# Ordering the norm chains' TensorE work behind later projection matmuls, in a two-layer diffusion backbone

## The chip, the cores and the metric

One core of a Trainium2 chip (trn2). The metric is the device time of one execution in microseconds (us). Engine names in the rows: PE is TensorE's matmuls, PEld its weight loads, DVE VectorE, ACT ScalarE, POOL GpSimd, SP SyncE, which issues the transfers.

## The reference, cut to what matters

512 latent tokens and 256 context tokens, 1024 features wide, pass two layers. Each layer is a mixer (layer 0: neighbourhood attention beside an mLSTM; layer 1: multi-head latent attention, MLA) and a gated ConvFFN, and each result is normalized twice: once as a sandwich norm of the branch, once as the norm that feeds the next projection.

```python
x = x + g1 * rms_norm(yx, norm_g[l, 1])
hx = modulate(rms_norm(x, norm_g[l, 2]), sh2, sc2)
x = x + g2 * rms_norm(conv_ffn(hx, ffn_w_up[l], ffn_conv_w[l], ffn_conv_b[l], ffn_w_down[l]), norm_g[l, 3])
...
def rms_norm(x, g):
    xf = x.astype(jnp.float32)
    y = xf * lax.rsqrt(jnp.mean(xf * xf, axis=-1, keepdims=True) + EPS)
    return (y * g.astype(jnp.float32)).astype(x.dtype)
```

The context tokens go through the same weights in layer 0, and only latent tokens leave layer 1.

## The kernel before, in words

Features lie on the partitions, in KD = 8 tiles of 128 (index k or m), tokens on the free axis. Every fp32 operand of a projection is split into a high and a low part, so each product is three matmuls: high weights (`whi`) by high data, high weights by low data, low weights (`wlo`) by high data. ACT makes `whi`, DVE `wlo`, from a transferred `wraw`.

The tokens of a projection are worked as segments: SX (512 latent columns) and SC (256 context columns) in layer 0's output projection and front of its FFN; SH[0] and SH[1] (256 latent columns each) and SC1 in the last part of layer 0's down projection and in layer 1. When all eight tiles of a segment are projected, its norm chain (`YNorm.chain`, L443; `RawNorm.chain`, L489) is put on a list, and the loops of the next segment trace a few of its steps after each of their own tiles (`step`, L381; `until`, L390, traces what is left). The chain of a segment is, in order:

1. column sums of squares over all features (`sums4`, L395, tiles `ysum` and `pss`, groups of four small matmuls; `pssy` for the wide segment);
2. ACT copies the sums (`srow`), four or two `psc` matmuls select and turn them (`sums_bc`, L405), DVE copies them to `rv`, POOL raises them to a power (`ry`), three short DVE instructions refine `ry`;
3. PE spreads `ry` over the partitions by transposes (`bcasts`, L367, `bcast`, L231), into `bcy` for the sandwich norm and `bcm` for the second norm;
4. for each k DVE scales the branch by `bcy` (a scalar_tensor_tensor on `acc`), DVE or POOL adds it to the stream (`x`), ACT squares, and after k = 3 and k = 7 four `pss` matmuls add up;
5. steps 2 and 3 again for `bcm`, and for each k DVE, ACT and in some k POOL make the high and low part `h` that the next projection reads.

A RawNorm chain (last down projection of layer 0) makes the unscaled `h` within its step 4, by ACT and DVE, and its `bcm` only gives a factor that is applied later.

Around the chains stand `yps` matmuls (output projection, L1195 to L1219), `puf` (the first up projections of an FFN, `front`, L1266), `pu` and `pd` (its steady middle), `pdl` (the last group of the down projection, L1325; its results go through PSUM tiles with two buffers and are added to `acc` by one DVE instruction each), and `qps`, `kps`, `kvp` (the projections of MLA). A scheduler of the language orders the instructions of every engine from what is traced and from its own estimate of times; each engine then runs its own list in that order. An order can be asked for between two instructions (`tc.issue_after`, used in `sums4`). In MLA the keys of a head are split into parts by `split_keys0`, the second head's after the first tile of scores of head 0 was traced (L1658).

Of the kernel before, what the change touches and what calls it, by code (L numbers as in the profile page):

```python
# [18 lines left out]
TX = 512  # L19
TC = 256  # L20
T = TX + TC
# [43 lines left out]
def hybrid_backbone_kernel(ctx: ExitStack, tc: tile.TileContext, *aps):  # L65
    nc = tc.nc
    V, S, G, PE = nc.vector, nc.scalar, nc.gpsimd, nc.tensor
    a = dict(zip(_DEV, aps))
    out = aps[len(_DEV)]
# [68 lines left out]
    def instr(i):  # L138
        return getattr(i, "ins", i)

    def mm(o, l, r, start, stop):
        return PE.matmul(out=o, lhsT=l, rhs=r, start=start, stop=stop)  # L142

    def tr(o, i):
        PE.transpose(out=o, in_=i, identity=ident[0:i.shape[0], 0:i.shape[0]])  # L145

    def act(o, i, func=AF.Copy, **kw):
        S.activation(out=o, in_=i, func=func, **kw)  # L148
# [41 lines left out]
    def proj(o, w, x, cols, ks=tuple(range(KD)), first=True, last=True):  # L190

        whi, wlo = w
        xhi, xlo = x
        for lo, hi, oo in cols:
            for k in ks:
                wh = whi[:, k * 128:(k + 1) * 128]
                wl = wlo[:, k * 128:(k + 1) * 128]
                oa = o[:, oo:oo + hi - lo]
                mm(oa, wh, xhi[:, k, lo:hi], first and k == ks[0], False)
                mm(oa, wh, xlo[:, k, lo:hi], False, False)  # L200
                mm(oa, wl, xhi[:, k, lo:hi], False, last and k == ks[-1])

    def proj_steps(o, w, x, cols):
        for c in cols:
# [24 lines left out]
        return y  # L229

    def bcast(o, col):  # L231
        tr(o, col.to_broadcast([128, 128]))

    def colsum(pss, sq, j, k, nk, first):
        mm(pss[:, j:j + 1], sq, ones_c, first, k == nk - 1)
# [131 lines left out]
    def bcasts(rs, n, name):  # L367
        bc = (ps_a if n > 4 else ps_c)("bc" + name)
        for j in range(n):
            bcast(bc[:, j * 128:(j + 1) * 128], rs[:, j:j + 1])  # L370
        return bc

    def sq_cols(pss, src, w, first, last):
        sq = sqp.tile([128, 512], F32, tag="sq", name="sq")
        act(sq[:, :w], src, AF.Square)
        for j in range(w // 128):
            mm(pss[:, j:j + 1], sq[:, j * 128:(j + 1) * 128], ones_c, first and j == 0, last and j == w // 128 - 1)

    chains = []

    def step(n):  # L381

# [7 lines left out]
    def until(sg):  # L390

        while any(c[0] == sg for c in chains):
            step(1)

    def sums4(ps, w, srcs, first, last):  # L395

        def one(i):
            return PE.matmul(out=ps[32 * i:32 * i + 32, 0:w], lhsT=ones32, rhs=srcs[i], start=first, stop=last,
                             tile_position=(0, 32 * i))
        n_ = len(srcs) - 1  # L400
        with tc.issue_after(instr(one(n_))):
            for i in range(n_):
                one(i)

    def sums_bc(ps, sg, name):  # L405

        row = scratch("srow")
        act(row[:, 0:sg.w], ps[:, 0:sg.w])
        psc = ps_c("psc")
        for j in range(sg.nt):  # L410
            mm(psc[:, j:j + 1], row[:, j * 128:(j + 1) * 128], sel4[:, 0:1], True, True)
        return rstd_bc(psc, sg.nt, D, name)

    class YNorm:
# [811 lines left out]
    def ffn(l, segs, osegs, parts, xs, h, accp, acc, Gt, groups, mod=None, done=lambda sg, k: None,  # L1226
# [5 lines left out]
        with ExitStack() as fs:  # L1232
# [58 lines left out]
            def down_mm(o, js, wu, m, sg):  # L1291
                for j in js:
                    whi, wlo = wu[j]
                    xh, xl = hid[j]
                    wh, wl = whi[:, m * 128:(m + 1) * 128], wlo[:, m * 128:(m + 1) * 128]
                    c0, c1 = sg.po, sg.po + sg.w
                    mm(o, wh, xh[:, c0:c1], j == js[0], False)
                    mm(o, wh, xl[:, c0:c1], False, False)
                    mm(o, wl, xh[:, c0:c1], False, j == js[-1])

            full = segs if pw > 512 else [Seg(n, 0, 0, 0)]

# [238 lines left out]
    with ExitStack() as l1b:  # L1541
# [112 lines left out]
                tt(V, h1lo[k], mixb[k], fr(h1hi[k]), ALU.subtract)  # L1654

        wv1 = wload(a["w_ukv"][1])
        for i, _ in enumerate(scores(0)):
            if i == 0:  # L1658
                for lo, hi in ((0, TX), (TX, T)):
                    split_keys0(1, lo, hi)  # L1660
            if i < 2:
                prep_q(i + 1)
            if i < NT // 2:
                prep_v(0, [i])
# [179 lines left out]
```

## Time and profile before

| | us |
|---|---|
| time, median of three runs | 1801.6 (1799.39 to 1803.42) |
| profiled execution | 1800.14 |
| its span, first to last instruction | 1798.2 |
| PE busy | 1732.4 (96%) |
| DVE busy | 1177.8 (66%) |
| ACT busy | 749.0 (42%) |
| POOL busy | 254.4 (14%) |
| mean granted clock of PE | 0.990 |

Busy time is the union of an engine's instructions. The views used are the page, the waits of an engine (who was waited for, in total, how often, and the longest), busy time by windows (with the granted clock), and the timeline, whose rows give the start, the duration, the instruction and in brackets the idle time ahead of it. A row of the timeline with x2 or x3 joins neighbours of one kind and gives their common duration. The span is 1.9 us shorter than the execution.

### The profile page before, as it was taken

To read this page: it belongs to the slowest core of one execution; us is meant where nothing else is said; L and a number is where in the kernel's file an instruction comes from. 1 tells how busy PE (TensorE), PEld (TensorE's weight loads), DVE (VectorE), ACT (ScalarE), POOL (GpSimd) and SP (SyncE) were. 2 spreads that over 40 slices of the span, in tenths; PEclk is the share of its full clock that TensorE was granted. 3 is DMA by queue.
4 is the path that set the end of the run, shared out by engine and by line. 5 is a ranking of instruction groups with operands and counts; after the bars stand their busy time and mean duration, and the time that the engine had idled before them with its cause. 6 is when DMAs were issued, how large, how long until landed. Compare 5 with 4: busy or idle time off the path is not lost.

```text
span 1798.2 us, 26707 instructions
## 1 busy us (share of the span) xinstructions
PE 1732.4 (96%) x10498; PEld 1454.3 (81%) x10498; DVE 1177.8 (66%) x2308; ACT 749.0 (42%) x1300; POOL 254.4 (14%) x304
## 2 busy tenths in 40 slices
PE   6999999999999999999999999999999999999997
PEld 4777877887878888888888878788878888888885
DVE  3384577559266686777764657788884574556555
ACT  3333345445344422232221335577784454333242
POOL 1000024225320000000000002344451200000001
PEclk8999999999999999999999999999999999999999
DMA  9344232113313343444331311000012133324221
GB/s 309 109 136 141 83 107 93 54 53 124 100 36 94 117 127 118 135 125 135 119 98 60 91 39 49 24 13 13 13 36 85 48 108 94 92 84 134 76 94 48
DMA packets 63261, 162.40 MB, mean 90 GB/s; under 512 B 6272, under 2 KB 19792, under 8 KB 63136
## 3 DMA queue, kind: packets, MB, share of 16 engines
q1 hardware_dynamic: 61616, 156.52, 27.7%
q0 software_dynamic: 1376, 4.04, 0.6%
q8 instruction: 83, 1.36, 0.3%
q14 instruction: 42, 0.34, 0.1%
q10 hardware_dynamic: 144, 0.13, 0.0%
HBM read 158.57 MB, written 2.10 MB: 89 GB/s over the span
## 4 chain that ended last, share of the span: by engine, by line
PE 70%; DVE 5%; ACT 2%; POOL 2%; issue 2%; DMA 1%; DVEq 0%; POOLq 0%; ACTq 0%
PE pu L142 29%; PE pd L142 14%; PE sp L142 4%; PE yps L142 4%; PE puf L142 3%; PE pdl L142 3%; PE pt L145 2%; PE qp L142 2%; PE ot L142 2%; PE vp L142 1%; PE kp L142 1%; DVE acc L157 1%; PE ops L142 1%; DVE wlo L151 1%; PE ptp L145 1%
## 5 line engine op out<-in xcount | busy, mean ns | idle before, releaser
L148 ACT ACTIVATE whi<-wraw 128x1024 fp32r<-128x1024 f32 x186 | 195.5, 1058 | 465.7 <-PE pu L142 210.0
L151 DVE TENSOR_TENSOR wlo<-wraw,whi 128x1024 fp32r<-128x1024 f32 x184 | 226.3, 1234 | 222.4 <-ACT whi L148 222.1
L142 PE MATMUL pu<-h,whi 128*128 128x256 f32 (+1 forms) x1280 | 315.4, 337 | 0.0
L142 PEld LDWEIGHTS pu<-h,whi 128*128 128x128 f32 x1280 | 219.8, 190 | 26.3 <-issue 1.0
L142 PE MATMUL pd<-hid,whi 128*128 128x512 f32 (+1 forms) x864 | 232.6, 357 | 1.6 <-DVE acc L151 1.5
L142 PE MATMUL pu<-h,wlo 128*128 128x512 f32 (+1 forms) x640 | 215.2, 336 | 0.0
L142 PEld LDWEIGHTS pd<-hid,whi 128*128 128x128 f32 x864 | 152.5, 189 | 28.2 <-DVE acc L151 3.9
L151 POOL TENSOR_TENSOR ry<-rv,mhalf 128x2 f32<-128x2 f32 (+2 forms) x26 | 24.2, 931 | 991.7 <-DVE rv L154 988.4
L142 PE MATMUL pd<-hid,wlo 128*128 128x512 f32 (+1 forms) x432 | 152.2, 354 | 0.0
L151 DVE TENSOR_TENSOR acc<-pd,acc 128x512 f32<-128x512 f32 (+1 forms) x192 | 109.8, 586 | 45.2 <-PE pd L142 44.3
L142 PEld LDWEIGHTS pu<-h,wlo 128*128 128x128 f32 x640 | 121.4, 190 | 12.7
L142 PE MATMUL pu<-hb,whi 128*128 128x512 f32 x304 | 118.3, 389 | 0.0
L142 PE MATMUL pu<-lb,whi 128*128 128x512 f32 x304 | 118.3, 389 | 0.0
L142 PE MATMUL pu<-hb,wlo 128*128 128x512 f32 x304 | 118.3, 389 | 0.0
L157 DVE SCALAR_TENSOR_TENSOR av<-aw,s,av 128x512 f32<-128x512 f32 x140 | 102.9, 750 | 19.7 <-DMA aw<-in_ada_w_dram 19.3
L154 POOL TENSOR_SCALAR P<-P,rl 128x768 f32<-128x768 f32 (+1 forms) x96 | 85.9, 896 | 148.1 <-DVE nm L154 56.7
L157 DVE SCALAR_TENSOR_TENSOR u<-pu,c_ffn_conv,u 128x511 f32<-128x511 f32 (+1 forms) x160 | 94.4, 611 | 10.0 <-ACT u L148 8.6
L142 PEld LDWEIGHTS pd<-hid,wlo 128*128 128x128 f32 x432 | 81.1, 188 | 11.8
L142 PE MATMUL sp<-kr,qh 128*128 128x256 f32 (+1 forms) x256 | 71.4, 353 | 1.3 <-ACT P L148 0.7
L148 ACT ACTIVATE u<-u 128x512 f32<-128x512 f32 (+2 forms) x46 | 32.7, 712 | 88.0 <-DVE u L157 76.3
L151 DVE TENSOR_TENSOR pTl<-pt,pTh 128x512 fp32r<-128x512 f32 x96 | 64.4, 682 | 5.5 <-ACT pTh L148 4.8
L142 PEld LDWEIGHTS pu<-hb,wlo 128*128 128x128 f32 x304 | 57.1, 188 | 11.9
(456 smaller groups left out, 3836.7 us busy)
## 6 DMA issues: line engine op xcount, KB each, us to landing
wraw<-in_ffn_up_dram SPq DMA_DIRECT2D x88, 512.0 KB, 3.6
aw<-in_ada_w_dram SPq DMA_DIRECT2D x112, 256.0 KB, 2.8
wraw<-in_ffn_down_dram SPq DMA_DIRECT2D x44, 512.0 KB, 3.6
aw<-in_ada_w_dram SPq DMA_DIRECT2D x40, 512.0 KB, 4.5
wraw<-in_w_in_dram SPq DMA_DIRECT2D x20, 512.0 KB, 3.7
wraw<-in_w_tok_dram SPq DMA_DIRECT2D x8, 512.0 KB, 4.2
wraw<-in_w_out_dram SPq DMA_DIRECT2D x8, 512.0 KB, 3.6
wraw<-in_w_o_dram SPq DMA_DIRECT2D x8, 512.0 KB, 3.5
```

The source lines that it names most:

```text
L142: return PE.matmul(out=o, lhsT=l, rhs=r, start=start, stop=stop)
L145: PE.transpose(out=o, in_=i, identity=ident[0:i.shape[0], 0:i.shape[0]])
L148: S.activation(out=o, in_=i, func=func, **kw)
L151: e.tensor_tensor(out=o, in0=x, in1=y, op=op)
L154: e.tensor_scalar(out=o, in0=x, scalar1=s1, scalar2=s2, op0=op0, op1=op1)
L157: V.scalar_tensor_tensor(out=o, in0=x, scalar=s, in1=y, op0=op0, op1=op1)
```

## The change

`mmp` takes the place of `mm` in `proj` and `down_mm`: it is the same matmul, and it counts its columns. `behind(i, cols)` registers a chain's instruction, if a chain is on the list; when the projection matmuls traced after it have summed to `cols` columns, the matmul at which that happens gets to stand ahead of the chain's instruction in PE's order (a dependence without a semaphore). The first matmul of a group of sums is put behind 3600 columns (14 matmuls of 256), the first `psc` behind 5280, the first broadcast of `bcy` or `bcm` behind 10800. `until` forgets what is still registered. The second head's key split is traced ahead of the scores of head 0. No arithmetic comes or goes.

```diff
--- before.py
+++ after.py
@@ -141,8 +141,28 @@
     def mm(o, l, r, start, stop):
         return PE.matmul(out=o, lhsT=l, rhs=r, start=start, stop=stop)
 
+    chains, pend = [], []
+
+    def behind(i, cols):
+
+        if chains:
+            pend.append([instr(i), cols])
+
+    def mmp(o, l, r, start, stop):
+
+        i = mm(o, l, r, start, stop)
+        n = 1
+        for d in r.shape[1:]:
+            n *= d
+        for p in pend:
+            p[1] -= n
+            if p[1] <= 0:
+                tc.add_manual_dep(p[0], instr(i).name, mybir.DependencyInfo(
+                    mybir.DependencyClass.NoSync, mybir.DependencyReason.DATA), reason="order")
+        pend[:] = [p for p in pend if p[1] > 0]
+
     def tr(o, i):
-        PE.transpose(out=o, in_=i, identity=ident[0:i.shape[0], 0:i.shape[0]])
+        return PE.transpose(out=o, in_=i, identity=ident[0:i.shape[0], 0:i.shape[0]])
 
     def act(o, i, func=AF.Copy, **kw):
         S.activation(out=o, in_=i, func=func, **kw)
@@ -196,9 +216,9 @@
                 wh = whi[:, k * 128:(k + 1) * 128]
                 wl = wlo[:, k * 128:(k + 1) * 128]
                 oa = o[:, oo:oo + hi - lo]
-                mm(oa, wh, xhi[:, k, lo:hi], first and k == ks[0], False)
-                mm(oa, wh, xlo[:, k, lo:hi], False, False)
-                mm(oa, wl, xhi[:, k, lo:hi], False, last and k == ks[-1])
+                mmp(oa, wh, xhi[:, k, lo:hi], first and k == ks[0], False)
+                mmp(oa, wh, xlo[:, k, lo:hi], False, False)
+                mmp(oa, wl, xhi[:, k, lo:hi], False, last and k == ks[-1])
 
     def proj_steps(o, w, x, cols):
         for c in cols:
@@ -229,7 +249,7 @@
         return y
 
     def bcast(o, col):
-        tr(o, col.to_broadcast([128, 128]))
+        return tr(o, col.to_broadcast([128, 128]))
 
     def colsum(pss, sq, j, k, nk, first):
         mm(pss[:, j:j + 1], sq, ones_c, first, k == nk - 1)
@@ -367,7 +387,9 @@
     def bcasts(rs, n, name):
         bc = (ps_a if n > 4 else ps_c)("bc" + name)
         for j in range(n):
-            bcast(bc[:, j * 128:(j + 1) * 128], rs[:, j:j + 1])
+            i = bcast(bc[:, j * 128:(j + 1) * 128], rs[:, j:j + 1])
+            if j == 0 and name in ("y", "m"):
+                behind(i, 10800)
         return bc
 
     def sq_cols(pss, src, w, first, last):
@@ -375,8 +397,6 @@
         act(sq[:, :w], src, AF.Square)
         for j in range(w // 128):
             mm(pss[:, j:j + 1], sq[:, j * 128:(j + 1) * 128], ones_c, first and j == 0, last and j == w // 128 - 1)
-
-    chains = []
 
     def step(n):
 
@@ -391,6 +411,7 @@
 
         while any(c[0] == sg for c in chains):
             step(1)
+        pend.clear()
 
     def sums4(ps, w, srcs, first, last):
 
@@ -398,7 +419,9 @@
             return PE.matmul(out=ps[32 * i:32 * i + 32, 0:w], lhsT=ones32, rhs=srcs[i], start=first, stop=last,
                              tile_position=(0, 32 * i))
         n_ = len(srcs) - 1
-        with tc.issue_after(instr(one(n_))):
+        head = one(n_)
+        behind(head, 3600)
+        with tc.issue_after(instr(head)):
             for i in range(n_):
                 one(i)
 
@@ -408,7 +431,9 @@
         act(row[:, 0:sg.w], ps[:, 0:sg.w])
         psc = ps_c("psc")
         for j in range(sg.nt):
-            mm(psc[:, j:j + 1], row[:, j * 128:(j + 1) * 128], sel4[:, 0:1], True, True)
+            i = mm(psc[:, j:j + 1], row[:, j * 128:(j + 1) * 128], sel4[:, 0:1], True, True)
+            if j == 0:
+                behind(i, 5280)
         return rstd_bc(psc, sg.nt, D, name)
 
     class YNorm:
@@ -1294,9 +1319,9 @@
                     xh, xl = hid[j]
                     wh, wl = whi[:, m * 128:(m + 1) * 128], wlo[:, m * 128:(m + 1) * 128]
                     c0, c1 = sg.po, sg.po + sg.w
-                    mm(o, wh, xh[:, c0:c1], j == js[0], False)
-                    mm(o, wh, xl[:, c0:c1], False, False)
-                    mm(o, wl, xh[:, c0:c1], False, j == js[-1])
+                    mmp(o, wh, xh[:, c0:c1], j == js[0], False)
+                    mmp(o, wh, xl[:, c0:c1], False, False)
+                    mmp(o, wl, xh[:, c0:c1], False, j == js[-1])
 
             full = segs if pw > 512 else [Seg(n, 0, 0, 0)]
 
@@ -1654,10 +1679,9 @@
                 tt(V, h1lo[k], mixb[k], fr(h1hi[k]), ALU.subtract)
 
         wv1 = wload(a["w_ukv"][1])
+        for lo, hi in ((0, TX), (TX, T)):
+            split_keys0(1, lo, hi)
         for i, _ in enumerate(scores(0)):
-            if i == 0:
-                for lo, hi in ((0, TX), (TX, T)):
-                    split_keys0(1, lo, hi)
             if i < 2:
                 prep_q(i + 1)
             if i < NT // 2:
```

The scheduler orders all engines anew under these rules. Line numbers of the changed kernel are some 20 higher (the matmul helper stays L142, transposes L145 become L165, the DVE helpers L151 and L157 become L171 and L177).

First place: DVE in the last down projection of layer 0, behind the broadcast `bcy` of SH[1]. `acc<-pdl,acc` is the addition that empties a PSUM tile of the running down projection; everything else belongs to the chain (`x`: addition to the stream; `h`: low part for MLA). Before, from the first step of the chain on:

```order
L157 SCALAR_TENSOR_TENSOR acc_4410<-acc_4410,G_0_4404,bcy 128x256
L151 TENSOR_TENSOR acc_4410<-pdl,acc_4410 128x256
L157 SCALAR_TENSOR_TENSOR acc_4410<-acc_4410,G_0_4404,bcy 128x256 x2
L157 SCALAR_TENSOR_TENSOR h_117<-x_4398,A_1_9641,h_116 128x256
L151 TENSOR_TENSOR x_4398<-acc_4410,x_4398 128x256
L151 TENSOR_TENSOR acc_4410<-pdl,acc_4410 128x256
L157 SCALAR_TENSOR_TENSOR h_117<-x_4398,A_1_9641,h_116 128x256
L157 SCALAR_TENSOR_TENSOR acc_4410<-acc_4410,G_0_4404,bcy 128x256
L157 SCALAR_TENSOR_TENSOR h_117<-x_4398,A_1_9641,h_116 128x256
L151 TENSOR_TENSOR x_4398<-acc_4410,x_4398 128x256
L157 SCALAR_TENSOR_TENSOR acc_4410<-acc_4410,G_0_4404,bcy 128x256
L151 TENSOR_TENSOR acc_4410<-pdl,acc_4410 128x256
```

Changed, after the first three `acc<-acc,G,bcy` and one `x` addition, which stand directly ahead of these rows:

```order
L177 SCALAR_TENSOR_TENSOR h_117<-x_4398,A_1_9641,h_116 128x256
L177 SCALAR_TENSOR_TENSOR acc_4410<-acc_4410,G_0_4404,bcy 128x256
L177 SCALAR_TENSOR_TENSOR h_117<-x_4398,A_1_9641,h_116 128x256 x2
L171 TENSOR_TENSOR x_4398<-acc_4410,x_4398 128x256
L177 SCALAR_TENSOR_TENSOR acc_4410<-acc_4410,G_0_4404,bcy 128x256 x2
L177 SCALAR_TENSOR_TENSOR h_117<-x_4398,A_1_9641,h_116 128x256
L171 TENSOR_TENSOR x_4398<-acc_4410,x_4398 128x256
L177 SCALAR_TENSOR_TENSOR h_117<-x_4398,A_1_9641,h_116 128x256
L177 SCALAR_TENSOR_TENSOR acc_4410<-acc_4410,G_0_4404,bcy 128x256
L177 SCALAR_TENSOR_TENSOR h_117<-x_4398,A_1_9641,h_116 128x256
L171 TENSOR_TENSOR x_4398<-acc_4410,x_4398 128x256
L171 TENSOR_TENSOR acc_4410<-pdl,acc_4410 128x256
```

Before, an addition that empties a tile stands in the second, sixth and twelfth row; in the changed order the first one after `bcy` stands behind seventeen instructions of the chain. On PE the `bcy` itself stands 32 `pdl` matmuls later than before, and between it and the first four `pss` matmuls of the chain stand 17 `pdl` and four `ysum` matmuls instead of 37 `pdl`.

Second place: PE in the front of layer 0's FFN, around the `bcm` of SC, the last broadcast ahead of the 256-column `puf` matmuls that read SC's `h`. Before, 15 `puf` matmuls of 512 columns stand between the two, of which these are the first:

```order
L142 MATMUL puf<-h_116,wlo 128x512
L142 MATMUL puf<-h_116,whi 128x512
L142 MATMUL puf<-h_117,whi 128x512
L142 MATMUL puf<-h_116,wlo 128x512
L145 MATMUL bcm<-c_ident,ry 128x128 x2
L142 MATMUL puf<-h_116,whi 128x512
L142 MATMUL puf<-h_117,whi 128x512
L142 MATMUL puf<-h_116,wlo 128x512
L142 MATMUL puf<-h_116,whi 128x512
L142 MATMUL puf<-h_117,whi 128x512
L142 MATMUL puf<-h_116,wlo 128x512
```

Changed (`adav` are the sums of a later layer's modulation):

```order
L142 MATMUL puf<-h_117,whi 128x512
L142 MATMUL puf<-h_116,wlo 128x512
L142 MATMUL puf<-h_116,whi 128x512
L165 MATMUL bcm<-c_ident,ry 128x128 x2
L142 MATMUL puf<-h_117,whi 128x512
L142 MATMUL puf<-h_116,wlo 128x512
L331 MATMUL adav<-av_5329,ones_v 32x128 x4
L331 MATMUL adav<-av_5330,ones_v 32x128 x4
L142 MATMUL puf<-h_116,whi 128x256 x2
L142 MATMUL adav<-c_sel,arow 128x8
L142 MATMUL puf<-h_117,whi 128x256
```

Two matmuls of 512 columns and nine short `adav` are left between `bcm` and the first matmul that reads SC's `h`. On DVE, four `u<-puf` convolution steps of 512 columns, one `u` product and one `hid` now stand ahead of SC's last `h` step; before, three of the convolution steps stood ahead of it and the rest behind.

In the other places where a `bcy` or `bcm` is moved, the number of 256-column matmuls between `psc` and it goes from 8 to 22, 22, 16 and 16 (layer 1's output projection: SH[0]'s `bcy` and `bcm`, SH[1]'s `bcy` and `bcm`), and from 10 to 22 in the last down projection of layer 1. In layer 0's output projection 41 `yps` matmuls stand between SX's `bcy` and its first `pss`, where 62 stood, and 29 between its `bcm` and the first `puf`, where 58 stood. On SP eight transfers `aw` of layer 1's modulation are issued among the up weights of layer 0, instead of after them.

## Rows read from the trace of the kernel before

**Rows 1.** The page: busy time, share of span, instructions by engine.

```profile
PE 1732.4 (96%) x10498; PEld 1454.3 (81%) x10498; DVE 1177.8 (66%) x2308; ACT 749.0 (42%) x1300; POOL 254.4 (14%) x304
```

**Rows 2.** Windows: busy time by engine, clock, DMA share, GB/s; layer 1's FFN.

```profile
1450.00:1750.00 300.00, 300.00 (x1325) 248.41 (x1324) 174.60 (x215) 113.03 (x143) 0.00 (x0) 1.00 0.31 97
```

**Rows 3.** PE's waits, layer 0, 482 to 554: total, times, longest.

```profile
PE bcm L145 <- DVE ry L157: 1.4, 2, 1.0
PE ysum L398 <- ACT ysq L148: 1.1, 1, 1.1
PE bcy L145 <- DVE ry L157: 0.9, 1, 0.9
```

**Rows 4.** PE's waits, last down projection of layer 0 into MLA, 1049 to 1152.

```profile
PE pss L398 <- ACT acc L148: 1.8, 3, 0.7
PE bcy L145 <- DVE ry L157: 1.1, 3, 0.4
```

**Rows 5.** PE's waits, layer 1's output projection and front, 1372 to 1435.

```profile
PE pss L398 <- ACT acc L148: 1.5, 2, 1.1
PE bcm L145 <- DVE ry L157: 1.3, 2, 0.7
PE bcy L145 <- DVE ry L157: 1.3, 2, 0.7
```

**Rows 6.** PE's timeline (start, duration, instruction, idle before): layer 0's chains.

```profile
488.06 0.65 PE L145 MATMUL bcy<-c_ident,ry 128*128 128x128 f32 x4 [0.90 <-DVE ry L157]
...
506.04 0.62 PE L145 MATMUL bcm<-c_ident,ry 128*128 128x128 f32 x4 [0.98 <-DVE ry L157]
...
537.18 0.40 PE L145 MATMUL bcm<-c_ident,ry 128*128 128x128 f32 x2 [0.47 <-DVE ry L157]
...
540.86 0.40 PE L142 MATMUL puf<-h,whi 128*128 128x256 f32 x2
...
552.78 0.28 PE L142 MATMUL puf<-h,whi 128*128 128x256 f32 x1
552.90 0.28 PE L142 MATMUL puf<-h,wlo 128*128 128x256 f32 x1
```

**Rows 7.** PE's timeline: SH[1] in layer 0, SH[0] in layer 1, the end.

```profile
1070.14 0.43 PE L145 MATMUL bcy<-c_ident,ry 128*128 128x128 f32 x2 [0.33 <-DVE ry L157]
...
1076.47 0.64 PE L398 MATMUL pss<-acc,ones 128*32 128x256 f32 x8 [0.67 <-ACT acc L148]
...
1386.10 0.60 PE L142 MATMUL psc<-sel,srow 128*128 128x1 f32 x4
...
1388.43 0.40 PE L145 MATMUL bcy<-c_ident,ry 128*128 128x128 f32 x2 [0.67 <-DVE ry L157]
...
1775.01 0.43 PE L145 MATMUL bcy<-c_ident,ry 128*128 128x128 f32 x2 [0.31 <-DVE ry L157]
```

**Rows 8.** DVE's timeline: chain steps of 512 and 256 columns, a key split.

```profile
492.91 1.40 DVE L157 SCALAR_TENSOR_TENSOR acc<-acc,G,bcy 128x512 f32<-128x512 f32 x2
...
537.62 1.26 DVE L157 SCALAR_TENSOR_TENSOR acc<-x1c,A,bcm 128x256 f32<-128x256 f32 x3
...
1070.69 0.48 DVE L157 SCALAR_TENSOR_TENSOR acc<-acc,G,bcy 128x256 f32<-128x256 f32 x1 [0.60 <-PE pdl L142]
...
1152.53 0.42 DVE L151 TENSOR_TENSOR kr<-kps,kr 64x256 fp32r<-64x256 f32 x1
...
1780.40 0.75 DVE L151 TENSOR_TENSOR x<-acc,x 128x256 f32<-128x256 f32 x2
```

**Rows 9.** POOL's timeline: SX's second addition, and its last low part.

```profile
492.47 1.67 POOL L151 TENSOR_TENSOR x<-acc,x 128x512 f32<-128x512 f32 x1 [0.23 <-DVE acc L157]
...
515.06 1.27 POOL L151 TENSOR_TENSOR h<-acc,h 128x512 fp32r<-128x512 f32 x1 [0.75 <-ACT h L148]
```

**Rows 10.** Windows, columns as in rows 2: a waiting stretch and the next.

```profile
1049.00:1053.18 4.18, 2.97 (x16) 1.99 (x16) 4.05 (x7) 2.63 (x3) 0.00 (x0) 1.00 0.13 8
1053.18:1056.59 3.41, 3.41 (x17) 3.41 (x17) 2.78 (x6) 0.42 (x1) 0.00 (x0) 0.50 0.38 144
```

## The prediction

> **What bounds the kernel now.** I read the page first: PE is busy 1732.4 of the span's 1798.2 us, DVE 1177.8, ACT 749.0 [rows 1]. The windows show where PE stands still: not at all in the steady middle of an FFN, 300.00 busy in 300 us [rows 2]. So time can only come from the stretches between, and PE's waits list them. They fall on norm chains: in layer 0's output projection and front `bcm` waits 1.4, `ysum` 1.1 and `bcy` 0.9 [rows 3]; from layer 0's last down projection into MLA `pss` waits 1.8 and `bcy` 1.1 [rows 4]; in layer 1's output projection and front `pss` waits 1.5, `bcm` 1.3, `bcy` 1.3 [rows 5]; near the end one `bcy` waits 0.31 [rows 7]. The timeline then gives the distances that a chain needs: from `psc` to the broadcast it feeds 1388.43 - 1386.10 = 2.3 us, wait included [rows 7].
>
> **Unit prices.** A 256-column projection matmul starts 0.12 behind its neighbour and lasts 0.28 [rows 6]; a 512-column one costs 300/1325 = 0.23 [rows 2]. As an interrupted stream must drain and fill again, each stall also loses 0.28 - 0.12 = 0.16 that the list of waits doesn't show. A chain step on DVE costs about 0.40 for 256 columns (1.26 for three, 0.48 of which is the last one's own length) and an addition 0.34 (0.75 for two); a 512-column step 0.66 [rows 8].
>
> **What the change can remove.** Layer 0's front half: 1.4 + 1.1 + 0.9 = 3.4 in four stalls, 3.4 + 4 x 0.16 = 4.0. Into MLA: 1.8 + 1.1 = 2.9 in six stalls, 3.9. Layer 1: 1.5 + 1.3 + 1.3 = 4.1 in six stalls, 5.1. End: 0.31 + 0.16 = 0.5. Together 13.5, if every such wait went and nothing came.
>
> **What it puts in their place.** Work of a chain is not less; PE matmuls put ahead of one link are missing behind it. A chain's length per link is set by DVE, ACT and POOL, so each place is a comparison of two lists that run side by side from a broadcast on.
>
> *SH[1] in layer 0's last down projection.* Before, 37 `pdl` filled the space between `bcy` and the first `pss`, and even so `pss` came 1076.47 - 1070.14 = 6.33 us later with a wait of 0.67 [rows 7]. In the changed order 17 `pdl` and the four `ysum` stand there: 0.2 for the broadcast, 17 x 0.12 and 0.6 for a group of four sums (0.64 with its end, rows 7), 2.8 us. On DVE seventeen chain instructions, fourteen steps of some 0.40 and three additions of 0.34, now stand ahead of the first addition that empties a `pdl` tile: 0.55 from `bcy` to the first step [1070.69 - 1070.14, rows 7, 8], plus 14 x 0.40 + 3 x 0.34 = 6.6, plus the addition's own 0.4, together 7.5 us. There are two such tiles, so the third tile's matmuls wait for it; PE without stalls is there at 2.8 + 0.6 for the `pss` = 3.4. PE thus loses 4.1, first at `pss`, then at `pdl`; with two resumptions 4.4. At most 6, if DVE also waits for ACT's high parts; at least 2.5, if DVE's list runs some steps ahead of the price above.
>
> *The other chains there.* Two `bcm` keep a distance of 11 matmuls from their `psc`: 1.3 and 1.1 plus 0.2 for `psc`, against 2.3: 0.8 + 1.0. Before, other work stood between. With 0.2 for one `pss`: 2.0, between 0.5 (if the adjoining `ysum` delay the `psc` anyway) and 3.
>
> *End.* The same effect at the last down projection: behind SH[0]'s `bcy` eleven chain instructions stand ahead of the first emptying addition, seven of 0.40 and four of 0.34: 0.55 + 4.2 + 0.4 = 5.1. PE is at the third tile after 0.2 + 17 x 0.12 + 0.6 = 2.8. Loss 2.3, with the resumption 2.4, between 1 and 3.
>
> *Layer 0's output projection.* SX's `bcy` to first `pss`: before 62 `yps`, now 41, so 0.4 + 41 x 0.12 = 5.3. POOL's second addition ended 494.14, which is 6.08 after `bcy` at 488.06 [rows 6, 9]; DVE had a weight split in front then, 0.5, and a square still follows. Loss about 1.1. From `bcm` to the first `puf` 29 `yps` instead of 58: 3.75 us, and the products of k = 5 follow 15 x 0.23 later, at 7.5 with the broadcast's 0.3. POOL ended that k's low part 516.33 - 506.04 = 10.3 after `bcm` [rows 6, 9]; by DVE's steps ahead of it (eight of 0.66 = 5.3) and POOL's own three it could be 9.0. Loss 1.5 to 2.8, I take 2.2. Together 3.3, between 1 and 5.
>
> *Layer 0's front.* From SC's `bcm` to the first reader of its `h` 540.86 - 537.18 = 3.7 before [rows 6]; now 0.2 + 2 x 0.23 + nine short `adav`, which no row here prices: 0.5, and 1.1 at the price of a 256-column matmul. DVE's list from `bcm` to the last `h`: sixteen instructions of SC less two on POOL, 14 x 0.40, four convolution steps of 0.66, two 512-column products that cost no more than such a step, and 0.5 at the start: 10.0. The last tile's first reader is the 42nd `puf`, so PE is there at 1.2 + 41 x 0.12 = 6.1. Loss 3.9, less 0.4 since the `adav` aren't due later: 3.5, between 2 and 5.
>
> *Layer 1.* Here the intended effect holds: between `psc` and its broadcast now 22, 22, 16 and 16 matmuls, 2.6 or 1.9 plus the `psc`'s 0.2 to 0.3, against 2.3. So `bcy` and `bcm` wait no more. But the first `pss` of SH[0] has 3.4 us behind `bcy` where it had about as much, and waits as before or longer. I leave 2.0 of the 5.1, between 0.5 and 3.
>
> *Edits at nothing.* The rules and the counts cost no instruction. Eight `aw` transfers stand among the up weights on SP; PE had no wait for a `pu` weight there, and each of these loads is prefetched. A weight that came late would cost at most one load's spacing, 2 us. The second head's key split is one DVE instruction of 0.42 that now stands ahead of a softmax step [rows 8]; the first queries wait on either anyway: 0, between -0.4 and 0.4.
>
> **Sum.** Against: 4.4 + 2.0 + 2.4 + 3.3 + 3.5 + 2.0 = 17.6. Less 13.5 leaves 4.1 more. The profiled execution took 1800.14 (its span 1798.2 and 1.9 around it), so 1804.2; the runs' median lies 1.5 above that execution, so 1805.7. The bounds of the terms sum to 7.5 and 25, which all at once are unlikely; half that distance each way gives -1 to +8, that is 1800.7 to 1809.5 for the forecast's own case.
>
> **Rivals.** *Gains kept.* The losses in layer 0, MLA and layer 1 don't come, because DVE and ACT, with no emptying additions between their steps, run chains faster than my prices. Only the two stalls counted from bare steps stay, 4.1 + 2.4 = 6.5 against 13.5: 7.0 less, 1794.6. For it: waits of 0.6 to 1.0 at a broadcast are of exactly the kind that 12 more matmuls cover. Against it: rows 7's 6.33 us is longer than the space that is left.
>
> *Cancelled.* Both sums are as large as each other; what was a wait at `bcy` is one at `pss` or `puf`. 1801.6, within 2.
>
> *Clock.* In one stretch of 4.18 us PE was busy 2.97, and in the 3.41 us behind it the granted clock was 0.50, 1.2 GHz: 17 matmuls instead of 3.41/0.12 = 28, so 11 x 0.12 = 1.4 lost [rows 10]. The new stall at SH[1] leaves PE busy about 3.4 of 7.5 us, the one at the end 2.8 of 5.1, the front's 6.1 of 10: each share is lower than that 0.71. If two of the three are answered so, 2.8 more: 1808.5. The Trainium skill (TensorE: Matmul & The Clock Gate, HAM oscillation — how this bites in real kernels) describes the fall as what long waits for a transfer do to a loop of matmuls; by that picture waits as short as these bring none, and the sum stays 1805.7. This trace bears the picture out only in part, since ahead of its fall PE waited 4.18 - 2.97 = 1.2 us in all.
>
> *It does not do what it says:* a chain instruction that the scheduler already had late isn't moved. The order shows that most are moved, so this is 1801.6 with little chance.
>
> **Chances.** Forecast 0.46, clock 0.20, cancelled 0.18, gains kept 0.13, not moved 0.03. This kernel's measurement can tell 0.2%, 3.6 us, from no change: slower is above 1805.2, faster below 1798.0. Slower: three fifths of the forecast's case (0.28), the clock's 0.20 and a little of the cancelled, 0.51. Faster: nearly all of gains kept, 0.12. The rest, 0.37, within. For 8 in 10 the range leaves out most of gains kept and the end of the clock's: 1799.0 to 1811.0.
>
> **What would show it.** In the changed profile: PE's waits at `bcy` and `bcm` gone in layer 1; between SH[1]'s `bcy` and its `pss` a wait of 2 to 3 us, then one of over 1 at `pdl` for DVE's `acc`; the same at the end, about 2.3; a wait over 1 at the `puf` of SC's last k for DVE's `h`; stretches of clock 0.50 behind these, if the clock's case holds. It is wrong if `pss` and `pdl` wait under 1 us each there, or if steps of DVE are much quicker when no additions stand between.

## The result, and the profile after

The changed kernel takes 1811.95 us (median of six runs, 1809.57 to 1814.16) against 1801.8 (six runs, 1799.39 to 1803.42): ratio 1.0061, 95% interval 1.0049 to 1.0073, 10 us slower. Run once more, later, it was 1808.91 against 1802.21, ratio 1.0040 (1.0026 to 1.0055). The ratios are given as recorded and can differ a little from the quotient of the two medians beside them. The direction was the forecast's; 1805.7 was too little, and 1811.95 lies just above the range's end of 1811.0.

The page of the changed kernel's profile (this execution took 1813.31, 13.2 more than the profiled one of before): the span, and the busy time of each engine [rows 1].

```profile
span 1811.2 us, 26713 instructions
PE 1739.8 (96%) x10498; PEld 1460.7 (81%) x10498; DVE 1175.5 (65%) x2308; ACT 749.6 (41%) x1300; POOL 252.5 (14%) x304
```

The work is the same on every engine. PE is "busy" 7.4 us longer with the same 10498 matmuls: some took longer, or overlapped their neighbours less, as the first one behind a wait does.

PE's waits in the four places, in the order of the program. Layer 0's output projection and front, 482 to 560 [rows 3]:

```profile
PE puf L142 <- ACT h L168: 1.8, 2, 1.1
PE puf L142 <- POOL h L171: 1.2, 2, 0.9
PE pss L419 <- ACT acc L168: 0.9, 1, 0.9
PE puf L142 <- DVE h L177: 0.8, 2, 0.5
PE psc L142 <- ACT srow L168: 0.5, 1, 0.5
PE adav L142 <- ACT arow L168: 0.4, 1, 0.4
```

From layer 0's last down projection into MLA, 1040 to 1175, the main waits that are new or changed [rows 4]:

```profile
PE pss L419 <- ACT acc L168: 2.5, 2, 2.2
PE pdl L142 <- DVE acc L171: 2.2, 1, 2.2
...
PE bcs L165 <- DVE sg L177: 1.2, 1, 1.2
PE bcm L165 <- DVE ry L177: 1.0, 2, 0.5
```

Layer 1's output projection and front, 1372 to 1450 [rows 5]:

```profile
PE ysum L419 <- ACT ysq L168: 0.9, 1, 0.9
PE pss L419 <- ACT acc L168: 0.8, 1, 0.8
PE puf L142 <- POOL lb L171: 0.8, 2, 0.5
PE puf L142 <- ACT whi L168: 0.4, 1, 0.4
```

At the end (1762 to 1812) a wait at `pdl` for DVE's `acc` has come:

```profile
PE pdl L142 <- DVE acc L171: 2.1, 2, 1.9
```

So the waits at `bcy` and `bcm` are gone in layer 1. In layer 0 most of them are now waits of the next link: `puf` waits for the `h` tiles, `pss` for the squares, `pdl` for its tile; two waits of 0.5 at `bcm` are new in the last down projection and MLA.

The second half of the story is in the windows with the granted clock (columns as in rows 2). These five stretches of the changed kernel between 550 and 1160 have a clock of 0.50, 1.2 GHz:

```profile
551.40:554.80 3.40, 3.40 (x17) 3.40 (x18) 2.82 (x6) 1.06 (x1) 0.00 (x0) 0.51 0.26 81
1060.00:1063.40 3.40, 3.40 (x19) 3.40 (x18) 2.37 (x6) 0.83 (x2) 0.00 (x0) 0.50 0.43 145
1087.33:1094.15 6.82, 6.22 (x31) 5.19 (x32) 2.81 (x8) 3.04 (x8) 0.00 (x0) 0.50 0.00 0
1148.78:1152.18 3.40, 3.40 (x18) 3.40 (x18) 1.81 (x10) 0.42 (x1) 0.81 (x2) 0.50 0.00 0
1155.60:1159.00 3.40, 3.40 (x8) 2.72 (x9) 2.21 (x4) 0.77 (x2) 2.29 (x3) 0.50 0.00 0
```

Before had only the second of them in this part [rows 10]. The first and the third stand right behind the new waits. What they cost is an estimate from the start distances in rows 2 and 6. At full clock the matmuls would start 0.12 apart: 3.40/0.12 = 28 where 17 ran, 11 x 0.12 = 1.3 lost; in the third 6.22/0.12 = 52 where 31 ran, 2.5 lost; in the fourth 10 x 0.12 = 1.2; in the fifth eight 512-column matmuls, 3.40 - 8 x 0.23 = 1.6. These four together make 6.6 us.

The length of each stretch, between the same two matmuls in either trace, named by their time before:

| stretch of before | before | changed | change | of it clock | waits | forecast |
|---|---|---|---|---|---|---|
| 484.1 to 553.4, layer 0's front half | 69.3 | 75.5 | +6.2 | 1.3 | +4.9 | +2.8 |
| 1045.0 to 1162.2, into MLA | 117.2 | 124.3 | +7.2 | 5.3 | +1.9 | +2.5 |
| 1372.1 to 1440.1, layer 1 | 68.0 | 65.9 | -2.1 | 0 | -2.1 | -3.1 |
| 1754.9 to 1784.6, the end | 29.7 | 31.3 | +1.5 | 0 | +1.5 | +1.9 |

Some 0.2 to 0.9 us of the first line comes back in the FFN behind it, as the `adav` sums needn't run there. The waits thus make about 6 us, the forecast's 4.1 with 2 more in layer 0; the clock makes the other half of this execution's 13. In the second profile of the changed kernel (1808.91, below) the same four stretches take 75.6, 119.7, 65.4 and 31.3; there the waits make some 4.5 us and the clock, worked out the same way, some 2.4. Of the 8.8 by which that execution was longer than the profiled one of before, 2.0 lie ahead of 484, where the order on PE is the same in both kernels.

### The profile page after: what moved, and what is told of

Its sections match the earlier page's. It is cut to its first block, busy times and chain, and to the rows that moved or that the text cites. A ratio compares the mean times of both kernels' runs of the same rounds, so it can differ in the third digit from the quotient of the medians.

```text
span 1811.2 us, 26713 instructions
## 1 busy us (share of the span) xinstructions
PE 1739.8 (96%) x10498; PEld 1460.7 (81%) x10498; DVE 1175.5 (65%) x2308; ACT 749.6 (41%) x1300; POOL 252.5 (14%) x304
## 4 chain that ended last, share of the span: by engine, by line
PE 69%; DVE 6%; issue 2%; ACT 2%; POOL 2%; DMA 2%; DVEq 0%; POOLq 0%; ACTq 0%
PE pu L142 27%; PE pd L142 13%; PE sp L142 4%; PE yps L142 4%; PE pdl L142 3%; PE puf L142 3%; PE qp L142 2%; PE pt L165 2%; PE ot L142 2%; PE vp L142 1%; DVE wlo L171 1%; PE kp L142 1%; DVE acc L177 1%; PE ops L142 1%; PE kvp L142 1%
## 5 line engine op out<-in xcount | busy, mean ns | idle before, releaser
L171 DVE TENSOR_TENSOR wlo<-wraw,whi 128x1024 fp32r<-128x1024 f32 x184 | 226.7, 1236 | 225.8 <-ACT whi L168 225.3
L142 PE MATMUL pu<-h,whi 128*128 128x256 f32 (+1 forms) x1280 | 315.5, 337 | 0.5 <-DVE u L177 0.5
L142 PEld LDWEIGHTS pu<-h,whi 128*128 128x128 f32 x1280 | 219.9, 190 | 26.9 <-issue 1.6
L142 PE MATMUL pd<-hid,whi 128*128 128x512 f32 (+1 forms) x864 | 232.6, 357 | 1.7 <-DVE acc L171 1.5
L142 PE MATMUL pu<-h,wlo 128*128 128x512 f32 (+1 forms) x640 | 215.2, 336 | 0.0
L142 PEld LDWEIGHTS pd<-hid,whi 128*128 128x128 f32 x864 | 152.6, 189 | 28.2 <-DVE acc L171 4.0
L171 POOL TENSOR_TENSOR ry<-rv,mhalf 128x2 f32<-128x2 f32 (+2 forms) x26 | 23.0, 884 | 990.6 <-DVE rv L174 984.2
L142 PE MATMUL pd<-hid,wlo 128*128 128x512 f32 (+1 forms) x432 | 152.2, 354 | 0.0
L171 DVE TENSOR_TENSOR acc<-pd,acc 128x512 f32<-128x512 f32 (+1 forms) x192 | 109.6, 585 | 45.3 <-PE pd L142 44.5
L142 PEld LDWEIGHTS pu<-h,wlo 128*128 128x128 f32 x640 | 121.3, 190 | 12.7
L142 PE MATMUL pu<-hb,whi 128*128 128x512 f32 x304 | 118.3, 389 | 0.0
L142 PE MATMUL pu<-lb,whi 128*128 128x512 f32 x304 | 118.3, 389 | 0.0
L142 PE MATMUL pu<-hb,wlo 128*128 128x512 f32 x304 | 118.3, 389 | 0.0
L177 DVE SCALAR_TENSOR_TENSOR av<-aw,s,av 128x512 f32<-128x512 f32 x140 | 102.8, 749 | 17.5 <-DMA aw<-in_ada_w_dram 16.6
L177 DVE SCALAR_TENSOR_TENSOR u<-pu,c_ffn_conv,u 128x511 f32<-128x511 f32 (+1 forms) x160 | 94.3, 610 | 10.0 <-ACT u L168 8.6
L142 PEld LDWEIGHTS pd<-hid,wlo 128*128 128x128 f32 x432 | 81.1, 188 | 11.7
L142 PE MATMUL sp<-kr,qh 128*128 128x256 f32 (+1 forms) x256 | 71.4, 353 | 1.1 <-ACT P L168 0.5
L142 PE MATMUL pdl<-hid,whi 128*128 128x256 f32 x320 | 65.3, 301 | 5.0 <-DVE acc L171 4.3
L171 DVE TENSOR_TENSOR pTl<-pt,pTh 128x512 fp32r<-128x512 f32 x96 | 64.3, 681 | 5.5 <-ACT pTh L168 4.8
```

The lines of the kernel that those rows point to most:

```text
L171: e.tensor_tensor(out=o, in0=x, in1=y, op=op)
L177: V.scalar_tensor_tensor(out=o, in0=x, scalar=s, in1=y, op0=op0, op1=op1)
```

## The experiments

**One place at a time.** The place where a chain instruction is traced decides whether the rules act. Each kernel had the changed kernel's order in that place, and the one of before elsewhere.

```diff
+    place, HELD = ["A"], 'A'          # 'C' for e2, 'D' for e3, 'T' for e5
     def behind(i, cols):
-        if chains:
+        if chains and place[0] in HELD:
             pend.append([instr(i), cols])
...
+                    place[0] = "CT"[l]     # ahead of the last down projection
...
+    place[0] = "D"                         # ahead of layer 1's output projection
```

The key split stood where it was before in these kernels. Layer 0's output projection and front:

> The order rules act only on the chains of layer 0's output projection and the front of its FFN; the key split stays where it was. Theory (waits moved, and the slow clock behind the new waits adds to them): 6 us slower, about 1808, with waits of PE at puf between 541 and 551 and one stretch of clock 0.50 of 3.4 us right behind them. Rival (waits alone, as the forecast's sum had it): 3 us slower, 1804.6, and no stretch of clock 0.50 there.

1806.26 against 1801.05: ratio 1.0025 (1.0015 to 1.0035), 5.2 us slower. Its profile has the same `puf` waits and, between 553.1 and 556.5, the slow stretch behind them; the stretch of layer 0 was 75.4 long, as in the changed kernel. And the slow stretch that before has at 1053 did not come in this execution, although nothing was changed there:

```profile
553.10:556.50 3.40, 3.40 (x18) 3.25 (x17) 2.71 (x7) 1.06 (x1) 0.00 (x0) 0.52 0.18 58
1050.00:1056.00 6.00, 5.09 (x32) 4.35 (x30) 4.34 (x9) 2.04 (x3) 0.00 (x0) 1.00 0.01 3
1056.00:1061.00 5.00, 3.74 (x19) 2.67 (x19) 4.87 (x9) 2.71 (x3) 0.00 (x0) 1.00 0.05 14
```

By time alone 2.7 to 6.3 us slower can't rule out the rival's 3; the rows decide: the stretch is 6.1 us longer, and a slow stretch stands in it. It costs about 1.5; the rest of the miss in this place is waits that were forecast too short. One slow stretch more or less, 1.5 us, is within what one kernel does from run to run.

Layer 0's last down projection and MLA's first projections:

> The order rules act only on the chains of layer 0's last down projection, which run on into MLA. Theory: 7 us slower, about 1809: two waits of 2.2 us at pss and pdl, and behind them 6.8 us of clock 0.50; the two further slow stretches of the changed kernel, near the start of MLA's heads, come back too, as they belong to this place. Rival one (waits alone): 2.5 us slower, 1804.3. Rival two (the later slow stretches belong to the key split or to the shift by layer 0's front): 4 to 5 us slower, with only the first 6.8 us of slow clock.

1805.46 against 1801.05: ratio 1.0023 (1.0011 to 1.0036), 4.4 us slower, and in a second run of the same kernel 1806.76 against 1800.49, 1.0041 (1.0029 to 1.0054). Two waits of 2.2, and 6.8 us of clock 0.50 right behind them, but full clock where the changed kernel had its two later slow stretches. The theory's 7 us was too much, and the time is rival two's. Its reason isn't shown: e6 below, with the key split and layer 0's front as before, has two slow stretches in that part as well. They come and go. Of the second run:

> The kernel of e2 once more, to stand beside e6_fill on the same chip. Both theories: 4 to 5 us slower than before, two waits of 2.2 us, slow clock behind them.

```profile
1055.40:1058.80 3.40, 3.40 (x18) 3.37 (x17) 2.77 (x6) 0.42 (x1) 0.00 (x0) 0.51 0.41 146
1082.70:1089.50 6.80, 5.70 (x28) 4.67 (x29) 3.31 (x9) 3.12 (x9) 0.00 (x0) 0.50 0.00 0
```

Layer 1's output projection and front:

> The order rules act only on the chains of layer 1's output projection. Theory: 2.5 us faster, about 1799.2, the waits at bcy and bcm in layer 1 gone, clock as before. Rival (a gain here is given back later, because the chains end no sooner): within 1 us of before.

1799.27 against 1801.05: ratio 0.9983 (0.9973 to 0.9993), 1.8 us faster by the medians, 3.1 by the ratio. `bcy` and `bcm` wait no more there; what is left of the waits is this:

```profile
PE pss L420 <- ACT acc L169: 0.8, 1, 0.8
PE puf L142 <- POOL lb L172: 0.8, 2, 0.5
PE ysum L420 <- ACT ysq L169: 0.5, 1, 0.5
PE puf L142 <- ACT whi L169: 0.4, 1, 0.4
```

The clock did not stay as before, and that part of the expectation was a miss. Right behind the `puf` waits, which before has not, stands a slow stretch:

```profile
1412.30:1415.70 3.40, 3.40 (x18) 3.40 (x18) 0.91 (x5) 1.19 (x2) 0.69 (x1) 0.50 0.46 165
```

The stretch of the table, 1372.1 to 1440.1, is 66.9 long here. It took 67.8 to 68.6 in the eight profiles with layer 1's old order, all at full clock there, and 65.4 to 65.9 in the three with the new order and full clock. So this order saves 1.9 to 3.2 us, and a slow stretch, where it comes, takes about half of it back.

The end alone:

> The rules act only on the last down projection of layer 1. Theory: 1.5 to 2 us slower, one wait of about 1.9 at pdl for DVE's acc in place of 0.31 at bcy. Rival (the end is set by the last chain alone, not by when its matmuls start): no change.

1803.93 against 1800.49: ratio 1.0019 (1.0009 to 1.0029), 3.4 us slower, more than the 1.5 to 2 expected. The wait itself was 1.9, as forecast, and one of the slow stretches of this execution stands right behind it, 16 matmuls in 3.4 us:

```profile
PE pdl L142 <- DVE acc L172: 1.9, 1, 1.9
```

```profile
1780.10:1783.50 3.40, 3.40 (x16) 3.40 (x17) 1.72 (x5) 0.83 (x2) 0.00 (x0) 0.51 0.48 161
```

The key split alone (no order rule acts, `HELD = ""`):

> No order rule acts; only the second head's key split is traced ahead of the scores of head 0. Theory: no change, within 0.5 us of 1801.8. Rival (the split delays the first softmax step and lets the clock fall at the start of MLA's heads): 2 to 3 us slower, with stretches of clock 0.50 between 1140 and 1155.

1800.23 against 1801.05: ratio 0.9994 (0.9982 to 1.0006): no change. Its profile has a slow stretch at 1149.6, where the rival expected one, another at 504.5, and none at 1053; so such stretches came at places where before had none, and cost nothing that the time shows. The five ratios less 1 add up to 0.25 + 0.23 - 0.17 + 0.19 - 0.06 = 0.44%, 8 us (0.62% with the second run of e2), beside 0.61 and 0.40% of the changed kernel: within their intervals, about 0.1% on each side for every one, the changed kernel is the sum of its parts.

**The waits filled.** Is the slow clock a price of the waits, or only near them? The kernel of e2 was given 18 matmuls in each of its two waits, in otherwise the same order on PE:

```diff
                 if k % 4 == 3:
-                    sums4(self.ps2, w, [y(k - 3 + i) for i in range(4)], k == 3, k == KD - 1)
+                    srcs = [y(k - 3 + i) for i in range(4)]
+                    if k == 3 and sg is SH[1]:
+                        wh_, xh_ = spare[0]        # operands of the last pdl
+                        for i in range(18):
+                            d = mm(self.ps[:, 512:768], wh_, xh_, True, True)
+                            if i == 0:
+                                behind(d, 9200)
+                        with tc.issue_after(instr(d)):
+                            last_ = sums4(self.ps2, w, srcs, True, False)
+                        with tc.issue_after(instr(last_)):
+                            for i in range(18):
+                                mm(self.ps[:, 512:768], wh_, xh_, True, True)
...
```

> The kernel of e2 (rules only in layer 0's last down projection), in the same order, with 18 matmuls of 256 columns put ahead of SH[1]'s first pss and 18 behind it, each set into one of the two waits of 2.2 us; their products go to unused columns of a PSUM tile and are never read. 18 x 0.12 = 2.16, so PE's other work keeps its times. Theory (the slow clock behind the waits is a price of its own): the 6.8 us of clock 0.50 behind them don't come, and the kernel is 2 to 3.5 us faster than e2_again, about 1802. Rival (only the waits cost, the clock is incidental): the same as e2_again, or up to 0.5 us slower for the added matmuls.

1805.74 against 1800.49: ratio 1.0028 (1.0018 to 1.0039), beside 1.0041 of e2_again on the same chip: 1.0 us less by the medians, 2.3 by the ratios, and the two intervals overlap. The profile shows that the filling did what it should there: both waits are gone, and the clock is full throughout and behind them. But this execution got two other slow stretches, at 1146.7 and 1157.0, where e2's had none:

```profile
1054.60:1058.00 3.40, 3.40 (x17) 3.40 (x17) 2.78 (x6) 0.42 (x1) 0.00 (x0) 0.50 0.42 145
1080.00:1090.00 10.00, 9.42 (x82) 7.46 (x82) 6.15 (x19) 5.60 (x16) 1.18 (x2) 1.00 0.01 2
1146.70:1150.10 3.40, 3.40 (x9) 2.57 (x9) 2.19 (x4) 1.01 (x2) 2.17 (x3) 0.50 0.02 5
1157.00:1160.40 3.40, 3.33 (x9) 2.78 (x10) 1.86 (x5) 1.98 (x4) 0.91 (x1) 0.50 0.01 2
```

The slow clock behind SH[1]'s waits is caused by them; that is shown in the rows. Its price is shown there too. From the first `pdl` behind the second wait to the next `bcm` both kernels run the same instructions in the same order on PE, e2_again at 1.2 GHz for most of it and e6 at full clock:

```profile
1083.80 0.80 PE L142 MATMUL pdl<-hid,whi 128*128 128x256 f32 x2 [2.23 <-DVE acc L172]
...
1091.95 0.40 PE L166 MATMUL bcm<-c_ident,ry 128*128 128x128 f32 x2 [0.51 <-DVE ry L178]
```

```profile
1083.04 0.51 PE L142 MATMUL pdl<-hid,whi 128*128 128x256 f32 x2
...
1088.85 0.40 PE L167 MATMUL bcm<-c_ident,ry 128*128 128x128 f32 x2 [0.51 <-DVE ry L179]
```

That is 8.15 us against 5.81: 2.3 us for 6.8 us of slow clock (the first 1.1 of which still fall into the wait), the low end of the 2 to 3.5 that I expected. The whole stretch 1045.0 to 1162.2 nevertheless takes 121.5 in e6 as in e2_again's 121.4, since the two other slow stretches take it back. So the rival, that only the waits cost, is wrong in this place; in the time of the kernel the gain can't be told from nothing. The same filling in the changed kernel, all rules acting:

> The changed kernel in its own order, all rules acting, with the filling of e6 in the two waits at SH[1] (18 matmuls of 256 columns in each, their products never read). Theory (slow clock is a price of its own, but waits elsewhere keep theirs): 1 to 3 us faster than after_again, a higher mean granted clock over its runs, no clock of 0.50 right behind SH[1]'s sums. Rival (waits alone): within 0.5 us of after_again.

> The changed kernel once more, to stand beside e8_fill_all on the same chip. Both theories: 10 us slower than before, two waits of 2.2 at SH[1].

1807.75 against 1802.21 (1.0037, 1.0024 to 1.0050), beside 1808.91 (1.0040, 1.0026 to 1.0055) of the changed kernel: 1.2 less, again not separable. Behind SH[1]'s sums the clock is full, and the same stretch from `pdl` to `bcm` takes 5.8 us, where the changed kernel's two profiles have 8.4 and 7.9. Other slow stretches came here too, at 1161.4 and 1792.9. The expected higher mean clock over the runs came, by little: 0.9874 against 0.9864.

The changed kernel's second profile is a test of its own. It has the same waits (2.2 at `pss`, 2.2 at `pdl`, 1.9 at the end), and full clock where the first profile had its second, fourth and fifth slow stretch; the stretch 1045.0 to 1162.2 is 119.7 long there and 124.3 in the first:

```profile
1058.00:1062.00 4.00, 3.09 (x20) 2.65 (x21) 3.92 (x8) 1.07 (x3) 0.00 (x0) 1.00 0.36 118
1085.70:1092.50 6.80, 5.00 (x25) 3.97 (x26) 4.02 (x11) 3.58 (x11) 0.00 (x0) 0.50 0.00 0
1144.00:1148.00 4.00, 3.48 (x30) 3.29 (x29) 3.02 (x11) 1.32 (x3) 1.67 (x2) 1.00 0.00 0
1151.00:1155.00 4.00, 3.00 (x11) 1.62 (x11) 3.51 (x7) 1.62 (x4) 3.15 (x4) 1.00 0.00 0
```

That is 4.6 us between two executions of one kernel. Over its seven runs on this chip the time goes in the main with the mean granted clock: 1805.14 at 0.989, 1808.91 at 0.987, 1812.61 at 0.983. Against the fifteen runs of before beside them it fell by 0.0024 (0.9889 to 0.9864), some 9 us more at 1.2 GHz; at 2.3 us for each 6.8 that is an estimate of 3 of the 6.7 us by which this run was slower.

**The sums held longer.** Whether the waits at `pss` and `pdl` are two or one:

```diff
-        behind(head, 3600)
+        behind(head, {'C': 10800}.get(place[0], 3600))
```

> As e2 (rules only in layer 0's last down projection), but the groups of sums are held behind 10800 columns instead of 3600. On PE the third tile's pdl matmuls then stand ahead of SH[1]'s first pss; DVE's list behind bcy is the same seventeen chain instructions. Theory (the two waits are one: DVE's list decides when PE gets a tile back): the wait at pss goes and the one at pdl grows from 2.2 to about 5, the time stays within 1 us of e2's, 1806. Rival (the sums, placed too early, are what stops PE): both waits go or shrink to 2.2 together, and the kernel is 2 us or more faster than e2.

```profile
PE pdl L142 <- DVE acc L172: 11.6, 2, 5.8
```

At SH[1] the wait at `pss` went and the one at `pdl` grew to 5.8, as the theory had it: DVE's list decides, and PE's order only sets where it waits. The time was a miss: 1811.21 against 1802.21, ratio 1.0047 (1.0031 to 1.0063), 9.0 slower and not e2's 4 to 6. I had looked at SH[1] only; in this order the next chain, SH[0]'s, has the second of the two waits, where e2 had none. And each of the two brought its own slow clock:

```profile
1080.83:1087.66 6.83, 5.16 (x26) 4.13 (x27) 3.98 (x11) 2.28 (x6) 0.00 (x0) 0.50 0.00 0
1104.72:1111.55 6.83, 4.36 (x26) 2.87 (x27) 4.36 (x12) 3.46 (x9) 0.00 (x0) 0.50 0.00 0
```

**A version that beats both.** The rules in layer 1 only, and SX's `bcy` alone held, by less:

```diff
-                behind(i, 10800)
+                behind(i, {'A': 4000}.get(place[0], 10800))     # in "A" for SX's bcy only
...
-                behind(i, 5280)
+                (behind(i, 5280) if place[0] == "D" else None)
```

> A version meant to beat both kernels: the rules act in layer 1's output projection and front, and in layer 0 only on SX's bcy, with 4000 columns instead of 10800, so that 16 matmuls stand between its sums and it instead of 8 and nothing else moves there. Theory: 2.1 us from layer 1 as in e3, and SX's wait of 0.9 with 0.16 more: 3 us faster, about 1798. Rival (SX's wait turns up later in its chain): 2 us faster, like e3.

1798.04 against 1800.49: ratio 0.9985 (0.9974 to 0.9996), 2.4 us faster than before. `bcy` waits no more in layer 0, but a `pss` now waits 0.4 there and the stretch became 0.5 shorter, not 0.9 or more: half of SX's wait turned up later, as the rival had it. By time e7 can't be told from e3, and its profile has e3's slow stretch in layer 1 too, at 1412.8.

## Why the prediction was right in kind and wrong in size

*SH[1]'s list against list.* Right, and close in size. The timeline of PE in the changed kernel:

```profile
1079.66 0.38 PE L165 MATMUL bcy<-c_ident,ry 128*128 128x128 f32 x2
...
1085.06 0.64 PE L419 MATMUL pss<-acc,ones 128*32 128x256 f32 x8 [2.23 <-ACT acc L168]
1087.93 0.79 PE L142 MATMUL pdl<-hid,whi 128*128 128x256 f32 x2 [2.23 <-DVE acc L171]
```

and of DVE, the first chain steps, two slower ones, and the addition that PE waits for:

```profile
1080.16 1.26 DVE L177 SCALAR_TENSOR_TENSOR acc<-acc,G,bcy 128x256 f32<-128x256 f32 x3 [0.71 <-PE bcy L165]
...
1082.04 0.60 DVE L177 SCALAR_TENSOR_TENSOR h<-x,A,h 128x256 fp32r<-128x256 f32 x1 [0.28 <-ACT h L168]
...
1084.87 0.77 DVE L177 SCALAR_TENSOR_TENSOR h<-x,A,h 128x256 fp32r<-128x256 f32 x1
...
1087.45 0.42 DVE L171 TENSOR_TENSOR acc<-pdl,acc 128x256 f32<-128x256 f32 x1
```

The two waits are 4.5 us where 4.1 was worked out, and e9 shows that they are one. PE got its tile back 1087.93 - 1079.66 = 8.3 after `bcy` where I had 7.5. Of the difference 0.3 is a wait of DVE for ACT's high part, which the bound named, and 0.4 are two `h` steps longer than the 0.40 that I took. Of the seventeen instructions four and not three are additions, which at my prices changes 0.06. The end is right too: 1.9 for 2.3. The two new waits at `bcm` there are 0.5 each, where the term of the other chains had 0.8 and 1.0.

*Layer 1.* Right in kind: no wait at `bcy` or `bcm`, and `pss` waits on as said. The stretch gained 2.1 and not 3.1 between the two first profiles, for one wait at `ysum` grew to 0.9 and `puf` waits 1.2 that weren't in the list of before; over all profiles with full clock it is 1.9 to 3.2.

*Layer 0's front half.* The right places, but 2 us too small. In the output projection I counted 1.1 at `pss`; 0.9 came. At `puf` PE waits 3.8 in six waits where I took 2.2 and 3.5, so these waits themselves are smaller than my terms; the one over 1, which was to be for DVE's `h`, came for ACT's. PE's listed idle time rose only from 3.6 in five waits to 5.6 in nine; yet the stretch lost 4.9 to waits. A wait costs more than its idle time, and the 0.16 for resuming I put on all waits that go, but in layer 0 on none that come. Even 0.16 is too little: in the changed kernel's timeline the matmul behind one lasts 0.39, and the next starts 0.22 behind it instead of 0.12:

```profile
546.62 0.39 PE L142 MATMUL puf<-h,whi 128*128 128x256 f32 x1 [0.28 <-DVE h L177]
546.84 0.28 PE L142 MATMUL puf<-h,wlo 128*128 128x256 f32 x1
```

That makes 0.26 a wait, 1.0 for the four more; `psc` and `adav` with waits of 0.5 and 0.4 were in no term, and the `adav` sums themselves stand in this stretch now. (Eight of the nine `adav` stand ahead of the first reader of SC's `h`; the ninth, behind two readers, has the wait of 0.4.) Some 1 us of it I can't assign to a row.

*The step that failed* is the clock: "If two of the three are answered so, 2.8 more", with a chance of 0.20, as a case beside the sum. The row it came from was read rightly, and so was the price of a slow stretch (1.4; 1.2 to 1.6 here). But the new wait of SH[1] was followed by 6.8 us at 1.2 GHz in four of four profiles that have it unfilled with the sums where the change put them (the changed kernel twice, e2 twice), the front's by 3.4 in four of four (the changed kernel twice, e1, e8), and the end's by 3.4 in two of four (e5, e8). Only for SH[1] is it shown that the waits cause it (e6, e8); in the other places it stands behind them and nothing more was tried. So the clock belonged in the sum, with 1.3 for the front and 2.5 for SH[1]: 4.1 + 3.8 = 7.9 more, 1809.5, and the range some 2 us higher. The Trainium skill (TensorE: Matmul & The Clock Gate, HAM oscillation — how this bites in real kernels) describes the fall as what long waits for a transfer do to a loop of matmuls. These rows are not of that kind: two waits of 2.2 with work between them were enough, and no transfer was waited for.

*The terms put at nothing* held: the key split alone changed nothing (e4), and the FFN in which the `aw` transfers moved took 491.4 us where it took 491.6.

*The range* failed by the run-to-run part of the same thing. Places such as 1053 and the start of MLA's heads (1148 and 1156 in the changed kernel's first profile) have a slow stretch in some executions and none in others, and so in kernels of another order (e4, e6, e8). In the changed kernel's first profile three such came, in the second none; between these two lie 4.6 us. Why its six first runs had a mean clock of 0.986 and a median 3 us above the seven later ones stays open.

## What to carry to other kernels

In layer 0 a wait of PE wasn't removed by putting later work ahead of the waiting instruction, since that instruction stands on a chain that is itself the longest list: what is put ahead is missing behind. Hold a link back by as much as its own latency needs (here 2.3 us from `psc` to broadcast, some 19 matmuls) and only where enough other work is left behind it, as in layer 1; and look what else the engine that serves the chain owes to the stream, here the additions that give PSUM tiles back. Where new waits of 2 us on TensorE are forecast, put the slow clock that follows into the sum.

## What the runs showed of the hardware that I had not expected

Two waits of 2.2 us with 0.6 us of sums between them were followed by 6.8 us at 1.2 GHz with 25 to 31 matmuls in them, which cost 2.1 to 2.6 us; with 36 matmuls of no use in the waits the clock stayed at 1.00. Much shorter waits also had a slow stretch behind them: those of 0.3 to 1.1 in layer 0's front in four of four profiles, those of 0.4 and 0.5 at layer 1's `puf` in two of five. And a kernel's slow stretches aren't its own alone: code that no kernel here changed had one near 1053 in six of the thirteen profiles (before, the changed kernel's first, both of e2, e6, e7) and full clock there in the other seven, the changed kernel's second among them.
